# Loading the decays later and splitting one weight copy in a decayed cumulative sum over a matmul

## The chip, the cores and the metric

The kernel runs on one core of one Trainium2 chip. The metric is the device time of one execution in microseconds, the median of several runs. Matrix products run on TensorE (PE, with its weight loads shown as PEld), the rest on VectorE (DVE), ScalarE (ACT) and GpSimd (POOL). Transfers between the chip's memory and the core's on-chip memory are issued by SP, ACT or POOL, each through a queue of its own, and carried out by 16 DMA engines.

## The reference

```python
B, S, D = (16, 2048, 1024)
xw = x @ w
out[:, 0, :] = xw[:, 0, :]
for t in range(1, S):
    out[:, t, :] = decay[None, :] * out[:, t - 1, :] + xw[:, t, :]
```

A matrix product of 32,768 rows with a 1024 x 1024 matrix, then along the time of each of the 16 sequences a running sum that is multiplied in each step by a factor of its column, the decay. All arrays are float32 in the chip's memory.

## The kernel before

Time is cut into chunks of 512 steps (`TL`), 64 in all, taken two at a time. The 1024 output columns are cut into 8 tiles of 128 (`n` = 0 to 7). A step of the outer loop computes one tile for one pair of chunks: 8 products (`k` = 0 to 7) over the 1024 input columns for each chunk, in bf16, into a tile `ps` in PSUM. Then the running sum is done by DVE, either directly from PSUM ("unpaired" tiles) or, for "paired" tiles, on every other time step with the square of the decay, where ACT and POOL prepare and finish the rest. DVE turns the result back to rows in `ot`, and SP issues the stores.

x comes in by POOL's queue, cast to bf16 (`load`, tile `xb`); DVE turns it in blocks of 32 x 32 (`turn`, tile `xw`), and ACT or DVE sorts it into `xt` (`part`). The weights lie in `wsb`, indexed by `k`, by tile `n` and by 128 columns. They come in four quarters, named by half `h` (tiles 0 to 3, or 4 to 7) and by `e` (even or odd `k`). A quarter is loaded into a staging area (`load_w`), then copied in four pieces, one for each `m` with `k = 2m + e` (`settle`); a piece covers the four tiles of its half, called slots below.

Almost every instruction is held in the order in which the program writes it (`pin`). The order is written out by hand in `agenda`: a string for each step, in which a letter with a number names a deed. The entry -99 runs before the first step. Its deeds are:

- `M0` to `M3`: load half chunks of x (POOL). `U0` to `U2`: load the second to fourth quarter of w (POOL). The first quarter is loaded at the very start by SP and ACT.
- `W` and `w`: copy one piece of w on DVE or ACT. 0 to 3 are the first quarter, 4 to 7 the second (half 0, odd `k`), 8 to 11 the third, 12 to 15 the fourth.
- `K0` to `K3`: matmuls that keep PE at work and wait for x's first parts.
- `E0` to `E15`: turn a part of a half chunk (DVE), four to a half chunk; so `E8` to `E11` are the third half chunk's turn, `E12` to `E15` the fourth's. `F` and `G`: sort one part into `xt` on DVE or ACT.
- `D` (`decays`): turn the decays from `rows` into columns, copy them to `dec`, and square them into `squares`, all on DVE. `rows` is filled by a memset (L329) and four small transfers on SP (L343 to L346), near the start of the program.
- `L`: the next load of x.

The deeds around the first steps that matter here: `p0` copies tile 0 out of PSUM on ACT, `g0` multiplies every other step of tile 0 by `dec` on ACT and is the first reader of `dec`; `p2` and `g2` do the same for tile 2; `W8` to `W11` follow on DVE in step 0's entry, `w12` to `w15` on ACT behind `g2`; `S1` and `S3` are the first scans on DVE.

In step 0 the loop writes the products of the first four tiles together: first the even `k` of chunk 0 in two halves, then the odd `k` in the order `k` = 1, 3, 5, 7 and for each of them the four tiles, each product a matmul of 512 columns at L131; then chunk 1. So the first matmul that reads w's second quarter is `k` = 1 of tile 0, and the next three are tiles 1 to 3 of the same `k`, which is the piece that `W4` copies.

Of the kernel before, what the change touches and what calls it, by code (L numbers as in the profile page):

```python
# [14 lines left out]
def _ap(ap_obj: bass.AP, new_ap, extra_offset=0):  # L15
    return dataclasses.replace(
        ap_obj,
        ap=[list(p) for p in new_ap],
        offset=ap_obj.offset + extra_offset,
    )  # L20
# [5 lines left out]
def kernel(  # L26
# [26 lines left out]
    nc = tc.nc  # L53
    pin = tc.keep_in_program_order
    B, S, D = x.shape
    assert w.shape == (D, D)

    NQ = 4
    P = 32
# [6 lines left out]
    R = K // 2  # L66
    CH = D // 2
    CR = CH // NQ
# [23 lines left out]
    wcols = wsb.rearrange("p k (h r) q i -> p k h q r i", h=2)  # L92
# [48 lines left out]
    class Tile:  # L141
# [39 lines left out]
        def copy(self):  # L181
            self.xs = sb.tile([128, 2 * TL], FP32, name=f"xs{self.lot % 3}")[:, 0:self.T]
            parts = self.ps if isinstance(self.ps, tuple) else (self.ps,)
            size = self.T // len(parts)
            for i, ps in enumerate(parts):
                pin(nc.scalar.copy(out=self.xs[:, i * size:(i + 1) * size], in_=ps))  # L186
# [93 lines left out]
    class Outlet:  # L280
# [8 lines left out]
        def store(self, b, t0):  # L289
# [4 lines left out]
            for j in range(0, self.nj, nj):  # L294
# [11 lines left out]
    stage = {(0, 0): room[0][:, 0:size],  # L306
             (0, 1): room[0][:, size:size * 3 // 2].bitcast(BF16),
             (1, 0): room[1][:, 0:size // 2].bitcast(BF16),
             (1, 1): room[1][:, size // 2:size].bitcast(BF16)}
# [8 lines left out]
    def settle(h, e, m, copy):  # L318
        src = stage[h, e][:, m * CH:(m + 1) * CH]
        pin(copy(out=wcols[:, 2 * m + e, h],  # L320
                 in_=src.rearrange("p (q r i) -> p q r i", q=NQ, r=R)))
# [3 lines left out]
    rows = const.tile([128, 2, P], FP32, name="rows")  # L325
    touch = const.tile([128, 1], BF16, name="touch")
    load_w((nc.sync, nc.scalar), 0, 0)
    pin(nc.vector.memset(idle, 0.0))  # L328
    pin(nc.vector.memset(rows, 0.0))  # L329
    pin(nc.scalar.copy(out=touch, in_=idle[:, 0:1]))  # L330

    gates = [const.tile([128, 128], BF16, name=f"gate{q}") for q in range(NQ)]
# [7 lines left out]
    spin(22, idle[:, 0:128])  # L340
    H = NJ // 2
    halves = ((0, H), (H, NJ))
    for q in range(NQ):  # L343
        pin(nc.sync.dma_start(
            out=rows[q * P:q * P + R],
            in_=_ap(decay, [[P, R], [CH, 2], [1, P]], q * CR)))  # L346
    cols = const.tile([128, 2, P], FP32, name="cols")

    def load_half(i):
# [10 lines left out]
    def part_one(i, copy):  # L360
        part(i // 8, copy, i % 4, i % 4 + 1, *halves[i // 4 % 2])

    def settle_one(i, copy):
        settle(i // 8, i // 4 % 2, i % 4, copy)

    def decays(i):
        pin(nc.vector.transpose(out=cols, in_=rows))
        pin(nc.vector.tensor_copy(
            out=dec.rearrange("p (h r) -> p h r", h=2), in_=cols[:, :, 0:R]))
        square(0)  # L370
# [64 lines left out]
    def turn_and_load(c):  # L435
# [13 lines left out]
        "x": lambda c: part(c, nc.vector.tensor_copy, 0, 2),  # L449
        "y": lambda c: part(c, nc.vector.tensor_copy, 2, M),  # L450
        "W": lambda i: settle_one(i, nc.vector.tensor_copy),
        "w": lambda i: settle_one(i, nc.scalar.copy),
        "M": load_half,
        "U": load_part,
        "E": lambda i: turn(i // 8, *halves[i // 4 % 2], i % 4, i % 4 + 1),
        "F": lambda i: part_one(i, nc.vector.tensor_copy),
        "G": lambda i: part_one(i, nc.scalar.copy),
        "K": spin_on,
        "D": decays,
        "d": square_again,  # L460
        "I": identity,
# [13 lines left out]
        "L": lambda i: load(*loads.pop(0)) if loads else None,  # L475
    }
    agenda = {
        -99: "M0 M1 U0 M2 M3 U1 U2 w0 W1 w2 W3 K0 K1 K2 K3 E0 E1 G0 E2 G1 E3 F2 G3 E4 E5 G4 E6 G5 E7 F6 G7 W4 w5 W6 W7 D E8 E9 G8 E10 G9 E11 F10 G11 E12 L E13 G12 L E14 G13 E15 L F14 G15",
        0: "p0 z0 W8 W9 W10 W11",
        1: "g0",  # L480
        2: "L S1 L",
# [194 lines left out]
```

## Time and profile before

The median of three runs is 904.1 us (904.0 to 904.33). The profiled execution has a span of 902.5 us from its first to its last instruction.

| | busy us | share of the span | instructions |
|---|---|---|---|
| PE (matmuls) | 896.7 | 99% | 4201 |
| PEld (weight loads) | 411.4 | 46% | 4201 |
| DVE | 824.2 | 91% | 632 |
| ACT | 686.9 | 76% | 958 |
| POOL | 656.6 | 73% | 755 |

Busy shares are means over the whole span. In this kernel the first 30 us differ from the rest: until about 15 us the engines wait for the first transfers. The granted clock of PE is full throughout (1.00 in every stretch but the last, 0.99). Lines of the timeline give the start in microseconds from the span's start, the length, the engine, the line of the program, the operation with what it writes and reads, how many instructions are merged in the line, and in brackets the idle time before it with what ended it. SPq, POOLq and PEq are the engines' issuing parts. The stretches of the trace around the change:

| stretch, us | PE busy | DVE busy | ACT busy | POOL busy |
|---|---|---|---|---|
| 5 to 10 | 5.00 | 1.04 | 1.80 | 2.73 |
| 10 to 15 | 4.82 | 3.25 | 3.41 | 4.48 |
| 15 to 20 | 4.72 | 2.85 | 2.18 | 4.10 |
| 20 to 25 | 5.00 | 2.64 | 3.25 | 3.68 |
| 25 to 30 | 5.00 | 4.89 | 3.91 | 4.89 |

### The profile page before, as it was taken

The page shows a single profiled execution, that of the slowest core. Times are in us where ns is not written, and L with a number is a line of the kernel's source. Part 1 is how long each engine was busy: PE and PEld are TensorE (multiplying, and loading weights), DVE is VectorE, ACT ScalarE, POOL GpSimd, SP SyncE. Part 2 cuts the span into 40 slices and gives each one's busy share as a digit, 9 for nine tenths or more (in the row PEclk, how much of TensorE's full clock was granted, in tenths as well). Part 3 has the DMA queues.
Part 4 walks back from the last instruction along what each step waited for, and adds up shares of the span by engine and source line. Part 5 has one row for each costly group of instructions (what it writes and reads, how often), then busy time and mean ns, then how long its engine had stood idle before and what let it go on. Part 6 is the DMA issues. An engine that isn't in the chain of part 4 may idle for free.

```text
span 902.5 us, 12285 instructions
## 1 busy us (share of the span) xinstructions
PE 896.7 (99%) x4201; PEld 411.4 (46%) x4201; DVE 824.2 (91%) x632; ACT 686.9 (76%) x958; POOL 656.6 (73%) x755
## 2 busy tenths in 40 slices
PE   9999999999999999999999999999999999999998
PEld 5544444444444444444444444444444444444444
DVE  4999998998999999999998999999999999999998
ACT  4889867777877877878778778777787787787743
POOL 7888678777767768777677687777777776876632
PEclk9999999999999999999999999999999999999999
DMA  9999999999999999999999999999999999999858
GB/s 193 194 215 220 231 231 206 215 231 243 251 249 248 242 251 246 244 250 253 227 236 228 221 228 230 232 227 227 232 230 228 227 234 223 228 226 218 183 142 236
DMA packets 403182, 204.77 MB, mean 227 GB/s; under 512 B 9392, under 2 KB 402096, under 8 KB 403120
## 3 DMA queue, kind: packets, MB, share of 16 engines
q1 hardware_dynamic: 265808, 134.77, 60.8%
q0 software_dynamic: 137024, 68.70, 56.8%
q8 instruction: 33, 0.54, 0.2%
q10 hardware_dynamic: 288, 0.52, 0.2%
q14 instruction: 29, 0.24, 0.1%
HBM read 138.42 MB, written 134.22 MB: 302 GB/s over the span
## 4 chain that ended last, share of the span: by engine, by line
PE 98%; DMA 1%; POOL 0%; issue 0%; DVE 0%; DVEq 0%; POOLq 0%
PE ps L131 96%; PE spare L131 1%; DMA xb<-in_x_dram 1%; DMA ot<-in_w_dram 1%; POOL ot L313 0%; PE spare L398 0%; PE ps L398 0%; DVE h L416 0%; DVE wsb L320 0%; DVEq L320 0%; POOLq L660 0%
## 5 line engine op out<-in xcount | busy, mean ns | idle before, releaser
L131 PE MATMUL ps<-xt,wsb 128*128 128x512 bf16 x4016 | 866.1, 378 | 0.5 <-DVE wsb L320 0.5
L131 PEld LDWEIGHTS <-wsb 128*128 128x128 bf16 x4152 | 405.9, 98 | 479.7 <-ACT wsb L320 0.8
L208 POOL TENSOR_TENSOR xs<-h,xs 128x512 f32<-128x512 f32 (+1 forms) x190 | 242.5, 1276 | 187.1 <-ACT h L169 85.5
L186 ACT COPY xs<-ps 128x1024 f32<-128x1024 f32 (+1 forms) x190 | 188.9, 994 | 152.8 <-PE ps L131 147.7
L272 DVE STREAM_TRANSPOSE ot<-so 128x1024 f32<-128x1024 f32 (+2 forms) x264 | 300.1, 1175 | 4.5 <-DMA out_dram<-ot 2.3
L260 POOL TENSOR_TENSOR so<-h,xs 128x512 f32<-128x512 f32 (+1 forms) x190 | 241.1, 1271 | 45.2 <-ACT h L169 28.0
L123 ACT COPY xt<-xw 128x2048 bf16<-128x2048 bf16 (+1 forms) x136 | 242.2, 1789 | 7.8 <-DVE xw L115 7.8
L105 POOL DMA_DIRECT2D xb<-in_x_dram x264 | 174.0, 660 | 3.5 <-DMA ot<-in_w_dram 1.1
L169 ACT ACTIVATE h<-so,dec 128x512 f32<-128x512 f32 (+1 forms) x190 | 145.4, 766 | 29.8 <-DVE so L213 26.7
L115 DVE STREAM_TRANSPOSE xw<-xb 128x2048 f32<-128x2048 f32 (+1 forms) x78 | 147.3, 1900 | 7.0 <-DMA xb<-in_x_dram 7.0
L213 DVE TENSOR_TENSOR_SCAN so<-spare,keep,xs 128x512 f32<-128x512 f32 (+1 forms) x97 | 119.8, 1237 | 25.7 <-POOL xs L208 25.4
L213 DVE TENSOR_TENSOR_SCAN so<-spare,xs 128x512 f32<-128x512 f32 x93 | 113.1, 1218 | 26.5 <-POOL xs L208 23.6
L169 ACT ACTIVATE h<-ps,dec 128x512 f32<-128x512 f32 (+1 forms) x189 | 129.4, 685 | 0.0
L233 DVE TENSOR_TENSOR_SCAN so<-dec,ps 128x1024 f32<-128x1024 f32 x34 | 76.7, 2259 | 1.0 <-ACT h L169 1.0
L233 DVE TENSOR_TENSOR_SCAN so<-dec,keep,ps 128x1024 f32<-128x1024 f32 (+2 forms) x35 | 75.4, 2153 | 0.0
L264 ACT COPY keep<-so 128x1 f32<-128x1 f32 x136 | 25.2, 188 | 9.4 <-DVE so L233 9.0
L204 ACT COPY so<-keep 128x1 f32<-128x1 f32 x97 | 18.5, 192 | 2.7 <-DVE ot L272 2.5
L131 PE MATMUL spare<-xt,wsb 128*128 128x512 bf16 (+1 forms) x56 | 11.9, 341 | 0.0
L131 PE MATMUL ps<-xw,wsb 128*128 128x256 bf16 (+1 forms) x68 | 11.2, 301 | 0.0
L202 POOL MEMSET so<- 128x1 f32 x93 | 10.6, 116 | 0.6 <-DVE ot L272 0.6
L313 POOL DMA_DIRECT2D ot<-in_w_dram x12 | 6.5, 544 | 3.2 <-DMA xb<-in_x_dram 2.1
L338 PE MATMUL spare<-idle 128*128 128x512 bf16 x22 | 7.5, 519 | 1.2 <-DVE idle L328 1.2
(39 smaller groups left out, 39.3 us busy)
## 6 DMA issues: line engine op xcount, KB each, us to landing
out_dram<-ot SPq DMA_DIRECT2D x236, 512.0 KB, 10.9
xb<-in_x_dram POOLq DMA_DIRECT2D x248, 256.0 KB, 7.9
out_dram<-ot SPq DMA_DIRECT2D x56, 128.0 KB, 2.6
xb<-in_x_dram POOLq DMA_DIRECT2D x16, 128.0 KB, 5.8
out_dram<-ot SPq DMA_DIRECT2D x8, 256.0 KB, 4.2
ot<-in_w_dram POOLq DMA_DIRECT2D x12, 128.0 KB, 5.1
out_dram<-xb SPq DMA_DIRECT2D x3, 256.0 KB
ot<-in_w_dram ACTq DMA_DIRECT2D x2, 256.0 KB, 5.1
```

Of the source, the lines that this page charges most:

```text
L105: pin(nc.gpsimd.dma_start(out=xb_of[c][quad(q), j0:j1], in_=_ap(x, [[D, P], [P * D, j1 - j0], [1, CQ]], (b * S + t0 + j0 * P) * D + q * CQ)))
L115: pin(nc.vector.transpose(out=dst.rearrange("p (m j i) -> p j m i", m=M, i=P)[:, j0:j1, m0:m1], in_=src.rearrange("p (j m c) -> p j m c", ...
L123: pin(copy(out=xt_of[c][:, m0:m1, :, j0 * P:j1 * P], in_=src))
L131: pin(nc.tensor.matmul(out=ps[:, t0:t1] if ps.shape[1] >= t1 else ps, lhsT=lhs, rhs=rhs, start=(k == 0 and t0 == start), stop=(k == K - 1),))
L169: pin(nc.scalar.activation(out=h, in_=src, func=mybir.ActivationFunctionType.Copy, scale=dec[:, self.n:self.n + 1]))
L186: pin(nc.scalar.copy(out=self.xs[:, i * size:(i + 1) * size], in_=ps))
L208: pin(nc.gpsimd.tensor_tensor(out=odds, in0=self.g, in1=odds, op=ALU.add))
L213: pin(nc.vector.tensor_tensor_scan(out=so[:, 3:T + 2:2], data0=squares[-1][:, n:n + 1].to_broadcast([128, T // 2]), data1=self.xs[:, 1:T:2 ...
L233: pin(nc.vector.tensor_tensor_scan(out=so[:, t + 2:t + 2 + size], data0=dec[:, n:n + 1].to_broadcast([128, size]), data1=ps, initial=befor ...
L260: pin(nc.gpsimd.tensor_tensor(out=self.so[:, 2:T + 2:2], in0=self.h, in1=self.xs[:, 0:T:2], op=ALU.add))
L264: pin(nc.scalar.copy(out=self.keep, in_=self.so[:, self.T + 1:self.T + 2]))
L272: pin(nc.vector.transpose(out=outlet.ot[:, :, c0:c0 + P], in_=self.so[:, 2 + t0:2 + t0 + nj * P].rearrange("p (i t) -> p i t", t=P)))
```

## The change

Two things are changed. First, the memset of `rows` and the four transfers of the decays become a deed `N`, which stands behind `F10`, that is behind the third half chunk's turn and its part on DVE; and `D`, which works the decays out, moves from behind `W7` to behind `F14`, the fourth half chunk's part on DVE. Second, the first piece of w's second quarter, `W4`, is copied on DVE in two instructions: `q4` copies slot 0 (128 of 512 elements a partition), `Q4`, behind it on DVE, slots 1 to 3. Between them in the string stands `w5`, which is on ACT.

```diff
-    pin(nc.vector.memset(rows, 0.0))
...
-    for q in range(NQ):
-        pin(nc.sync.dma_start(
-            out=rows[q * P:q * P + R],
-            in_=_ap(decay, [[P, R], [CH, 2], [1, P]], q * CR)))
+
+    def load_decay(i):
+        pin(nc.vector.memset(rows, 0.0))
+        for q in range(NQ):
+            pin(nc.sync.dma_start(
+                out=rows[q * P:q * P + R],
+                in_=_ap(decay, [[P, R], [CH, 2], [1, P]], q * CR)))
+
...
+    def settle_slots(i, r0, r1):
+        h, e, m = i // 8, i // 4 % 2, i % 4
+        src = stage[h, e][:, m * CH:(m + 1) * CH]
+        pin(nc.vector.tensor_copy(
+            out=wcols[:, 2 * m + e, h, :, r0:r1],
+            in_=src.rearrange("p (q r i) -> p q r i", q=NQ, r=R)[:, :, r0:r1]))
...
+        "N": load_decay,
+        "q": lambda i: settle_slots(i, 0, 1),
+        "Q": lambda i: settle_slots(i, 1, R),
...
-        -99: "M0 M1 U0 M2 M3 U1 U2 w0 W1 w2 W3 K0 K1 K2 K3 E0 E1 G0 E2 G1 E3 F2 G3 E4 E5 G4 E6 G5 E7 F6 G7 W4 w5 W6 W7 D E8 E9 G8 E10 G9 E11 F10 G11 E12 L E13 G12 L E14 G13 E15 L F14 G15",
+        -99: "M0 M1 U0 M2 M3 U1 U2 w0 W1 w2 W3 K0 K1 K2 K3 E0 E1 G0 E2 G1 E3 F2 G3 E4 E5 G4 E6 G5 E7 F6 G7 q4 w5 Q4 W6 W7 E8 E9 G8 E10 G9 E11 F10 N G11 E12 L E13 G12 L E14 G13 E15 L F14 D G15",
```

The order of the instructions on PE, ACT and POOL is the same as before. On ACT, `g0` now waits for DVE itself; before, an earlier wait of ACT on DVE covered the decays.

## The prediction

> **What bounds the kernel now.** I read the chain of waits first, in order of time, because the page gives PE 99% of it and only its start and its end can hold anything else.
>
> ```profile
> 1.31 6.52 DMA xb<-in_x_dram
> ...
> 8.12 0.55 POOL ot L313
> ...
> 9.91 4.90 DMA ot<-in_w_dram
> ...
> 14.93 0.30 DVE wsb L320
> 15.23 0.05 issue
> 15.28 0.82 PE ps L131 x3
> ...
> 43.33 830.69 PE ps L131 x3848
> ```
>
> Columns are start, length, what. From 15.28 us on the chain is PE alone until the tail at 898 us: what reaches PE before 15.28 us, or stalls it later, moves the end one for one, and nothing else does. The last thing before 15.28 is one copy of w's second quarter on DVE (14.93, 0.30), which waits for the transfer that lands at 14.81; that was issued when the first x transfer had landed, at 7.84 (1.31 + 6.52).
>
> The timeline of the first 45 us comes next (start, length, engine, line, what, idle before).
>
> ```profile
> 1.66 1.35 SPq L344 DMA_DIRECT2D rows<-in_decay_dram  x4
> ...
> 14.93 0.69 DVE L320 COPY wsb<-ot 128x512 bf16<-128x512 bf16 x3 [0.85 <-DMA ot<-in_w_dram]
> ...
> 15.28 0.82 PE L131 MATMUL ps<-xt,wsb 128*128 128x512 bf16 x3 [0.46 <-DVE wsb L320]
> 15.54 0.23 DVE L367 STREAM_TRANSPOSE cols<-rows 128x64 f32<-128x64 f32 x1
> ...
> 15.81 0.17 DVE L368 COPY dec<-cols 128x8 f32<-128x8 f32 x1
> ...
> 18.99 0.39 DVE L123 COPY xt<-xw 128x512 bf16<-128x512 bf16 x1
> ...
> 20.35 1.42 DVE L115 STREAM_TRANSPOSE xw<-xb 128x256 f32<-128x256 f32 x4 [0.97 <-DMA xb<-in_x_dram]
> ...
> 24.09 1.04 DVE L320 COPY wsb<-ot 128x512 bf16<-128x512 bf16 x4 [2.01 <-DMA ot<-in_w_dram]
> ...
> 24.32 0.69 ACT L169 ACTIVATE h<-ps,dec 128x512 f32<-128x512 f32 x1
> ...
> 25.19 1.01 ACT L186 COPY xs<-ps 128x1024 f32<-128x1024 f32 x1 [0.18 <-PE ps L131]
> ...
> 28.90 1.19 PEld L131 LDWEIGHTS <-wsb 128*128 128x128 bf16 x7 [0.35 <-ACT wsb L320]
> ```
>
> To be seen: PE stands 0.46 us (14.82 to 15.28) for that copy, its only stall on real work. DVE has two holes, 0.97 us before 20.35 and 2.01 us before 24.09. The first reader of the decays, `g0` on ACT, starts at 24.32. ACT then works in a row to the four weight copies for which PE's weight loads wait until 28.90; the matmuls from 25.86 on stay 0.216 us apart (72 in 15.73), so these copies are just in time and ACT has no slack there beyond the 0.18 us of idle before 25.19.
>
> **The change, part by part.** The profiled execution has a span of 902.5 us; the runs' median of 904.1 us lies 1.6 us above it, and I take those 1.6 as unchanged.
>
> *The split copy.* `W4` (512 elements a partition) becomes `q4` (128) and `Q4` (384). Seven such bf16 copies on DVE took 283 to 428 ns, median 286; the shortest copy on DVE, 8 elements (L368), took 171. The line through these two is 0.228 ns an element, so `q4` is 0.20 us and `Q4` 0.26. PE's first matmul waits for slot 0 alone and starts 0.09 us sooner, at 15.19. The second needs `Q4`. The three copies in 0.69 us start 0.20 apart ((0.69 - 0.28) / 2); with `q4` 0.09 shorter, `Q4` starts 0.11 after it and ends at 14.93 + 0.11 + 0.26 = 15.30; with the 0.05 of issue it is ready at 15.35, and the second matmul is due at 15.19 + 0.216 = 15.41. So all 0.09 counts, with 0.06 to spare. Bounds: a `q4` as short as the memset of 64 elements (0.112) would let PE start 0.17 sooner, but `Q4` at 15.35 - 0.09 = 15.26 is then close behind, so 0.17 is the most; a `Q4` as long as the slowest copy (428 ns) is ready at 15.52, against 15.50 for the second matmul before, a loss of 0.02. I take the line, 0.09, since its ends are of this very kind of copy. `W6` and `W7` slip by 0.11 us; their matmuls come 1.7 and 2.6 us after the first, so this is covered. `w5` on ACT doesn't move.
>
> That 428 ns copy ran while POOL issued x transfers at 24.26. [...]
>
> *The decays leave the front.* Four transfers of 1 KB leave SP's queue at 1.66. In the trace's packet records they are 32 packets of 128 B, median 26 ns, at 5.21 to 6.98 us, among the first x packets, which begin at 5.28. That is 32 x 26 = 0.83 us of engine time: 0.05 us if spread over 16 engines, 0.21 if on 4. x's first landing, the transfers behind it and 14.93 come sooner by this; between 0 (a packet in a gap costs nobody) and 0.21 I take 0.05, the even spread. The memset of `rows` (0.11 us) leaves DVE at 1.10; the gates behind it are first needed at 8.31, so nothing.
>
> *`D` leaves DVE at 15.54* (transpose 0.23, copy 0.17, square 0.17, ending at 16.19). The next DVE work waits for x until 17.65: nothing.
>
> *`N`, the load.* The memset (0.11) goes into the hole from 19.38 to 20.35, covered. It releases SP at some 19.6, whose queue holds nothing until the stores at 38.79. Four issues take 1.35 us as before, the last starting near 20.6.
>
> *When they land* the trace doesn't show for this place. From below: w's first packet left SP's empty queue 1.02 us after its issue (0.75 to 1.77), so 20.6 + 1.0 + 0.1 = 21.7. Under load: the first store's first packet came at 42.59, 3.80 after its issue began, 2.14 of it the issue itself (6.42 / 3), so 1.7 after the issue's end; that puts the first decay packet at 19.6 + 0.35 + 1.7 = 21.65, and if the four then spread as before (5.21 to 7.03, 1.82 us) the last is in at 23.5. From above: the last decay transfer before took 4.3 us from issue to its end (2.7 to 7.03), giving 24.9, though w's 512 KB stood ahead in its queue; an x transfer of 128 KB takes 5.8, giving 26.4. The new place has a loaded machine but an empty SP queue, nearest to the store: I take 22.9, between the first two.
>
> [...]
>
> *`D` behind `F14`.* It can start when `F14` ends, 22.08, or when the decays land. It fills 0.65 us of the hole before 24.09. Behind it on DVE stand `W8` to `W11`, then the scans. `W8` can slip: PE needs it at 25.86 and it ends at 24.4.
>
> *The deadline.* `g0` gets a wait of its own on DVE. From landing to `dec` is 0.44 us (15.54 to 15.98) plus about 0.08 on either side, 0.60 in all. `g0` may start at 24.32 + 0.18 of ACT's idle time - 0.14 by which PE now runs sooner = 24.36. So decays that land by 23.75 cost nothing; each later microsecond is one that `g0`, the next two copies out of PSUM, `w12` to `w15` and PE lose in turn. At 22.9 there is 0.85 us of cover.
>
> Sum: -0.09 - 0.05 = -0.14 us, which gives 902.4 for the span and **903.95 us** for the time.
>
> **The rivals.**
>
> *The gain is swallowed, 904.1 us.* `Q4` comes late (the 428 ns case) or the x transfers land as before. For it: the spread of the copy's times. Against it: the median of the seven is 0.286. Its price is between -0.05 and +0.02. [...]
>
> *The decays are late, slower.* The mechanism is SP's small packets among POOL's big ones at 20 to 24 us; the place is ACT at 24.36; it decides from a landing at 23.75 on, and undoes the gain from 23.9. At 24.9 it costs 1.15 - 0.14: 905.1 us. At 26.4 it is 2.65 - 0.14: 906.6. Above 0.2% (905.9) it needs a landing at 25.7, over 5 us after the last issue. For it: the 4.3 us of the same transfer at the start. Against: that queue was full, and 1 KB is 8 packets of 26 ns.
>
> *The whole gap closes, 903.65 us.* Transfers that land sooner by the 0.21 bound and more, plus the short copy, let PE go on at 14.82. No more is there: this stall has 0.46 us, so faster by over 0.2% (below 902.3) has no mechanism in the profile.
>
> **How the numbers follow.** The forecast gets 0.58, the swallowed gain 0.15, late decays 0.19 (0.06 of it beyond 905.9), the closed gap 0.05, what I don't see 0.03. The range takes the forecast with its bounds and late decays up to the 4.3 us row: 903.6 to 905.1. A measurement of this kernel tells about 0.2% (1.8 us) from no change, so all but the far end of late decays is "the same": faster 0.02, same 0.91, slower 0.07.
>
> **What would show it.** The split: PE's stall at 15.28 shrinks from 0.46 to about 0.37, and PE's second matmul follows 0.22 after the first; a gap there is `Q4` late. The front: x's first wait ends some 0.05 sooner. The decays: the transpose of `rows` starts near 23.0 and `dec`'s copy ends before 24.3, with no idle time before `g0` put down to DVE. I am wrong if DVE waits for `rows` beyond 23.9, or if PE idles between 25.8 and 30 us.

## The result, and the profile after

The changed kernel takes 906.45 us (median of 11 runs, 905.0 to 907.81), the kernel before 904.1 us in the same comparison (903.81 to 904.48): a ratio of 1.0026, 95% interval 1.0018 to 1.0034. It is slower by 2.35 us, and its runs lie 2.8 us apart where those before lay within 0.7. The profiled execution has a span of 904.7 us, 2.2 above the 902.5 before.

The timeline of the changed kernel, with the columns as before:

```profile
14.77 0.36 DVE L372 COPY wsb<-ot 128x128 bf16<-128x128 bf16 x2 [0.84 <-DMA ot<-in_w_dram]
...
15.03 0.82 PE L131 MATMUL ps<-xt,wsb 128*128 128x512 bf16 x2 [0.35 <-DVE wsb L372]
...
19.33 1.28 SPq L346 DMA_DIRECT2D rows<-in_decay_dram  x4
...
24.56 0.24 DVE L377 STREAM_TRANSPOSE cols<-rows 128x64 f32<-128x64 f32 x1 [2.61 <-DMA rows<-in_decay_dram]
...
25.25 0.69 ACT L169 ACTIVATE h<-ps,dec 128x512 f32<-128x512 f32 x1 [1.09 <-DVE dec L378]
...
25.43 2.13 DVE L320 COPY wsb<-ot 128x512 bf16<-128x512 bf16 x4
...
25.99 1.46 PE L131 MATMUL ps<-xt,wsb 128*128 128x512 bf16 x5 [0.22 <-ACT h L169]
26.07 1.34 POOL L208 TENSOR_TENSOR xs<-h,xs 128x512 f32<-128x512 f32 x1
...
27.62 4.70 PE L131 MATMUL ps<-xt,wsb 128*128 128x512 bf16 x20 [0.17 <-DVE wsb L320]
...
29.55 2.49 PEld L131 LDWEIGHTS <-wsb 128*128 128x128 bf16 x13 [0.41 <-ACT wsb L320]
```

The same timeline some 10 us later:

```profile
36.67 2.27 DVE L115 STREAM_TRANSPOSE xw<-xb 128x2048 f32<-128x2048 f32 x1
...
40.92 1.02 PE L131 MATMUL ps<-xt,wsb 128*128 128x512 bf16 x4 [0.41 <-ACT xt L123]
...
42.73 1.02 PE L131 MATMUL ps<-xt,wsb 128*128 128x512 bf16 x4 [0.78 <-ACT xt L123]
```

In the kernel before, the lines that belong to the two readings below, POOL's first addition and chunk 2's turn, were:

```profile
26.45 1.30 POOL L208 TENSOR_TENSOR xs<-h,xs 128x512 f32<-128x512 f32 x1
...
34.24 2.27 DVE L115 STREAM_TRANSPOSE xw<-xb 128x2048 f32<-128x2048 f32 x1
```

PE's stall for the second quarter is shorter, 0.35 us, and ends at 15.03, 0.25 sooner than before. From there on it goes wrong. The decays are issued at 19.33, and DVE waits 2.61 us for them, until 24.56. ACT's `g0` starts at 25.25 where it started at 24.32. Behind the decays on DVE stand the four copies of w's third quarter; they start at 25.43 instead of 24.09, and take 2.13 us where they took 1.04, while POOL does an addition. That addition begins at 26.07, 0.38 us sooner than before, since POOL's loads ran sooner too (the one ahead of it ended at 25.98 for 26.34). And chunk 2's turn on DVE, which began at 34.24, begins at 36.67, so that PE waits for ACT's `xt` at 40.92 and 42.73, long after the decays are in.

The chain of waits of the changed kernel, in order of time (start, length, what), runs through the same places:

```profile
20.32 4.12 DMA rows<-in_decay_dram
...
24.56 0.26 DVE cols L377
...
25.43 2.13 DVE wsb L320 x4
27.56 3.32 DVE so L233 x2
...
36.75 2.20 DVE xw L115
...
40.78 1.90 ACT xt L123
...
50.23 9.88 PE ps L131 x45
```

Before, the chain was PE alone from 15.28 us; now it is the decays' transfer, then DVE until 39 us, then ACT's `xt` until 42.7, and only then PE.

How the loss divides is read from PE's weight loads, which are the same 4201 in the same order in both traces. The 131st starts 0.25 us sooner than before (23.87 against 24.12), the 161st 0.64 later (29.56 against 28.92), the 225th 2.15 later (44.88 against 42.73), the 4001st still 2.15. So 0.25 was gained by 15 us, 0.89 lost between 24 and 30 us, and 1.51 between 40 and 43: -0.25 + 0.89 + 1.51 = 2.15.

### The profile page after: what moved, and what is told of

It is laid out like the page before. It is cut to its first block, busy times and chain, and to the rows that moved or that the text cites. A ratio compares the mean times of both kernels' runs of the same rounds, so it can differ in the third digit from the quotient of the medians.

```text
span 904.7 us, 12204 instructions
## 1 busy us (share of the span) xinstructions
PE 892.3 (99%) x4119; PEld 410.8 (45%) x4201; DVE 826.1 (91%) x633; ACT 686.4 (76%) x958; POOL 656.5 (73%) x755
## 4 chain that ended last, share of the span: by engine, by line
PE 94%; DMA 2%; DVE 2%; issue 1%; POOL 0%; ACT 0%; SPq 0%; DVEq 0%; POOLq 0%
PE ps L131 93%; DMA xb<-in_x_dram 1%; PE spare L131 1%; DVE so L233 1%; DMA rows<-in_decay_dram 0%; DVE xw L115 0%; POOL ot L313 0%; DVE wsb L320 0%; ACT xt L123 0%; POOL xb L105 0%; DVE ot L272 0%; DVE so L213 0%; PE spare L408 0%; PE ps L408 0%; SPq L346 0%
```

## The experiments

Each was compared with the kernel before on its own chip, whose medians there were 904.32 (first four), 904.37 (next four) and 904.47 us (last three). "Moved" and "split" below are the two halves of the change.

**The split alone.** The agenda of before, with `q4 w5 Q4` for `W4 w5`:

```diff
-... G7 W4 w5 W6 W7 D E8 ...
+... G7 q4 w5 Q4 W6 W7 D E8 ...
```

> Only the split copy; the decays are loaded and worked out where they were before. Theory (the loss is all in the late decays; the split alone gives PE its 0.09 us): 904.0 us, 0.1 below before, PE's stall for the first piece of the second quarter some 0.09 us shorter. Rival (the split harms the copies behind it): above before.

904.22 us against 904.32, ratio 0.9998 (0.9989 to 1.0007). The split does no harm, and a gain of 0.1 us can't be told from none by the time. The traces can tell it a little better: from the start of the first copy to the first matmul behind it, it took 0.35 us before, 0.25 in the changed kernel and 0.31 here.

**The move alone.** The changed kernel with `W4` whole:

```diff
-... G7 q4 w5 Q4 W6 W7 E8 ...
+... G7 W4 w5 W6 W7 E8 ...
```

> Only the decays are moved, the copy is whole. Theory (late decays): the whole loss is here, 906.0 to 907.0 us, with DVE's transpose of the decays waiting for their transfers until about 24.5 us and runs that scatter over 1 us and more. Rival (loss from the split): 904.0.

907.83 us (906.5 to 908.21), ratio 1.0035 (1.0022 to 1.0047): the whole loss is here, and more than expected. Its timeline shows where the rest comes from:

```profile
25.14 3.73 DVE L320 COPY wsb<-ot 128x512 bf16<-128x512 bf16 x4
...
26.21 1.30 POOL L208 TENSOR_TENSOR xs<-h,xs 128x512 f32<-128x512 f32 x1
...
27.45 1.30 POOL L105 DMA_DIRECT2D xb<-in_x_dram  x2
28.76 1.30 POOL L208 TENSOR_TENSOR xs<-h,xs 128x512 f32<-128x512 f32 x1
...
28.93 12.71 PE L131 MATMUL ps<-xt,wsb 128*128 128x512 bf16 x58 [1.77 <-DVE wsb L320]
```

The four copies of the third quarter take 3.73 us; they end 0.12 us after POOL has done an addition and two issues of x loads in a row. The same copies as one group of the tile `wsb` (minimum, median and maximum in ns, then first and last start), in the kernel before, the changed one, and here:

```profile
L320 DVE COPY wsb<-ot x4: 286/290/428, 24.1 to 24.7; 128x512 bf16<-128x512 bf16 x4
```

```profile
L320 DVE COPY wsb<-ot x4: 275/359/1376, 25.4 to 26.2; 128x512 bf16<-128x512 bf16 x4
```

```profile
L320 DVE COPY wsb<-ot x4: 274/300/3091, 25.1 to 25.8; 128x512 bf16<-128x512 bf16 x4
```

One copy of the four, the last, is stretched from 0.29 us to 1.38 or 3.09. Before, the copies ran while POOL only issued loads, and ended at 25.13, well before POOL's addition at 26.45. In the changed kernel the meeting is close: the addition begins at 26.07, the last copy at 26.2, and without the hold the copies would have ended near 26.47 (an estimate, 25.43 + 1.04).

**The load in front, the work late.** The decays are loaded as before, `D` stands behind `F14`, the copy is whole:

```diff
-... W6 W7 D E8 ...  ... L F14 G15
+... W6 W7 E8 ...  ... L F14 D G15
```

> The decays are loaded at the front as before, but worked out behind the fourth half chunk's turn; the copy is whole. Theory (what costs is the landing, not the place of the three instructions on DVE): 904.1 us, no change, runs within 0.7 us. Rival (0.65 us of work in that hole of DVE's delays the third quarter's copies): 904.5 and more.

904.18 us, ratio 0.9999 (0.9990 to 1.0008), runs 903.98 to 905.29. The place of the three instructions costs nothing that the time shows; what costs is the landing.

**The load earlier.** The changed kernel with `N` behind `W7`:

```diff
-... Q4 W6 W7 E8 E9 G8 E10 G9 E11 F10 N G11 ...
+... Q4 W6 W7 N E8 E9 G8 E10 G9 E11 F10 G11 ...
```

> The whole change, but the load stands right behind the second quarter's copies, some 3.6 us earlier on DVE. Theory (late landing): the transfers land near 20 us, before the transpose can start at 22, so nothing waits, and what is left is the split and the empty front: 903.85 us, 0.25 below before. Rival (small transfers among the big ones take longer the earlier they are issued, since more is queued, and land at the same time as in the changed kernel): 906 us.

904.16 us against 904.32 (runs 903.78 to 904.5), ratio 0.9996 (0.9987 to 1.0005). The loss is gone, and of the gain that is left 0.16 us is seen, which can't be told from none. From its timeline:

```profile
15.76 1.29 SPq L346 DMA_DIRECT2D rows<-in_decay_dram  x4
...
21.90 0.23 DVE L377 STREAM_TRANSPOSE cols<-rows 128x64 f32<-128x64 f32 x1
...
24.09 0.69 ACT L169 ACTIVATE h<-ps,dec 128x512 f32<-128x512 f32 x1
```

The transpose has no idle time before it. The packet records put the decays' packets at 19.15 to 20.71 us, 3.4 to 4.95 after the first issue; in the changed kernel it was 22.48 to 23.94, 3.15 to 4.6 after it. The delay goes with the issue, and is no property of one place.

**The decays behind the weight copies.** The changed kernel with `D` taken from behind `F14` and set behind `W11`; the load stays late:

```diff
-0: "p0 z0 W8 W9 W10 W11",
+0: "p0 z0 W8 W9 W10 W11 D",
```

> The whole change, but the decays are worked out on DVE behind W8 to W11 instead of ahead of them; the load stays late. Theory (the decays' lateness costs PE 0.9 us by way of ACT, and all beyond that comes from what stands behind the wait on DVE): W8 to W11 run near 24 us in about 1 us as before, g0 starts no sooner than 25.2, and the time is 904.6 to 905.2 us. Rival (the wait of ACT alone makes the loss, whatever DVE does): 906.0 and more.

905.21 us (904.82 to 905.99), ratio 1.0009 (1.0000 to 1.0018): 0.84 us above before, at the upper end of what was expected.

```profile
24.68 1.04 DVE L320 COPY wsb<-ot 128x512 bf16<-128x512 bf16 x4 [2.27 <-DMA ot<-in_w_dram]
...
25.64 0.23 DVE L377 STREAM_TRANSPOSE cols<-rows 128x64 f32<-128x64 f32 x1
...
26.30 0.69 ACT L169 ACTIVATE h<-ps,dec 128x512 f32<-128x512 f32 x1 [1.58 <-DVE dec L378]
...
27.03 16.25 PE L131 MATMUL ps<-xt,wsb 128*128 128x512 bf16 x70 [0.71 <-ACT h L169]
```

The copies take 1.04 us again, although `g0` starts a whole microsecond later than in the changed kernel (PE itself was some 0.5 us later here by its 131st weight load). PE never waits for `xt`. The trace is of the slowest of the 11 runs, 905.99: in it PE loses 1.39 us between its 131st and 161st weight loads and nothing behind them. By the medians, then, the wait on ACT makes 0.84 of the 2.35 us at most, less than half, and the rest comes from what stands behind the wait on DVE.

**The load later still.** `N` behind `E13`:

```diff
-... F10 N G11 E12 L E13 G12 ...
+... F10 G11 E12 L E13 N G12 ...
```

> The whole change, with the load two pieces of the fourth half chunk's turn later on DVE, some 1.7 us. Theory (PE loses what the landing is late, one for one): the transpose of the decays starts near 26.2 us and the time is 907.5 to 909 us. Rival (the landing is set by POOL's big transfers and not by the issue): 906.5, the same as the changed kernel.

908.05 us (five runs, 906.61 to 908.22), ratio 1.0036 (1.0024 to 1.0049). The transpose starts at 26.91, 2.35 later than in the changed kernel for an issue 1.71 later (21.04 against 19.33). The number came out as expected, yet not by that theory alone: the copies here escape POOL's addition (the longest takes 0.29 us), although the last of them began at 28.19, beside an addition that began at 28.17; there it is the addition that took longer, 1.45 us for 1.30. And something new appears. PE stands idle for 2.42 us until 28.14. The stretches after it follow; a line gives the stretch, its length, the busy time and number of instructions of PE, PEld, DVE, ACT and POOL, and then PE's granted clock (0.57 in the first line):

```profile
28.00:29.00 1.00, 0.64 (x2) 0.33 (x4) 1.00 (x4) 1.00 (x3) 0.83 (x1) 0.57 1.44 194
29.00:30.00 1.00, 1.00 (x3) 0.40 (x3) 1.00 (x1) 1.00 (x3) 1.00 (x2) 0.50 1.46 198
30.00:31.00 1.00, 1.00 (x4) 0.30 (x2) 1.00 (x2) 1.00 (x3) 0.99 (x3) 0.50 1.45 197
31.00:32.00 1.00, 1.00 (x5) 0.41 (x4) 0.89 (x2) 0.73 (x3) 1.00 (x1) 0.72 1.44 195
32.00:33.00 1.00, 1.00 (x6) 0.46 (x5) 1.00 (x1) 0.00 (x0) 1.00 (x3) 1.00 1.44 194
```

PE ran at half its clock until 31.5 us. So this run is no clean measure of the slope from landing to time.

**POOL's addition out of the way.** The changed kernel with `j0`, the first addition, behind POOL's next two loads of x. Nothing else moves in the program:

```diff
-3: "p2 z2 L g2 j0 S3 w12 w13 L w14 L w15 k1",
+3: "p2 z2 L g2 S3 w12 w13 L w14 L w15 j0 k1",
```

> The whole change, with POOL's first addition (j0) moved behind POOL's next two loads of x. Theory (the last of the third quarter's copies on DVE is held up by POOL's addition, since the late decays push the copy into it): no copy there takes over 0.6 us, DVE's first scan starts near 26.5 instead of 27.5, runs scatter less, and the time is 905.0 to 905.8 us. Rival (DVE is late by the wait alone, the long copy only shows it): 906.5 and the same long copy.

905.32 us (905.05 to 905.76), ratio 1.0011 (1.0002 to 1.0020). Against the kernel before it loses 0.95 us where the changed kernel lost 2.35, and its runs are 0.7 us apart instead of 2.8. The same group of copies:

```profile
L320 DVE COPY wsb<-ot x4: 275/341/422, 25.7 to 26.5; 128x512 bf16<-128x512 bf16 x4
```

No copy is held, DVE's first scan starts at 26.81 instead of 27.48, and yet the decays land no sooner (the transpose starts at 25.08). In this trace, of the slowest of the 11 runs, PE still waits 0.4 us for `xt`. The kernel before with `j0` later was not run, so what that move is worth without late decays is not known.

**One transfer of four.** The changed kernel with `for q in range(1)` in `load_decay`: three quarters of the decays stay zero.

> The whole change, but only the first of the four transfers of the decays is made: three quarters of the decays are left at zero. Theory (the wait under load before the first packet and the spread of the four add up to the late landing): the one transfer is in near 22.9 us, the transpose starts by 23.4, and the time is 903.7 to 904.3 us. Rival (the whole delay is before the first packet): the transpose starts at 24.2 or later and the time is 905.5 and more.

904.26 us against 904.37, ratio 0.9999 (0.9991 to 1.0008). From its timeline:

```profile
19.71 0.30 SPq L346 DMA_DIRECT2D rows<-in_decay_dram  x1
...
23.80 0.25 DVE L377 STREAM_TRANSPOSE cols<-rows 128x64 f32<-128x64 f32 x1 [1.55 <-DMA rows<-in_decay_dram]
...
24.40 0.69 ACT L169 ACTIVATE h<-ps,dec 128x512 f32<-128x512 f32 x1
24.46 0.90 DVE L320 COPY wsb<-ot 128x512 bf16<-128x512 bf16 x4
```

The transpose came later than expected (23.80, not 23.4), 4.1 us after the issue, and still all is well: `g0` is on time, and the copies end at 25.36, before POOL's addition. A landing 0.76 us sooner than in the changed kernel (23.80 against 24.56) is worth 2.5 us of time (2.35 lost there, 0.11 gained here, each against the kernel before on its chip). So the loss is not one for one; around here it is much steeper.

**Three on one chip.** The changed kernel and the move alone once more, and the move alone with `j0` later:

> The changed kernel once more, on one chip with the next two. Theory (the loss above 1 us hangs on how long POOL shuts out the last of the third quarter's copies, which differs from run to run): 905.5 to 907.5 us with runs 2 us apart, and in the profile the last copy's length again far from 0.29 us. Rival (scatter of the landing alone): runs within 1 us.

> The decays moved, the copy whole, once more. Theory (the split matters by its 0.1 us only, and the larger loss of the first such run came from the chip and the collision): within 0.7 us of the changed kernel's median on this chip. Rival (the split takes a microsecond off the loss): 1 us or more above it.

> The decays moved, the copy whole, and POOL's first addition (j0) behind its next two loads of x. Theory (POOL's addition and not the split decides): 905.2 to 905.9 us, runs within 1 us, no copy of the third quarter over 0.6 us. Rival: as the kernel with the decays moved alone.

The changed kernel again: 906.78 us (905.01 to 908.03), ratio 1.0026 (1.0017 to 1.0036); its last copy took 1.38 us. The move alone: 906.51 us (905.13 to 907.73), ratio 1.0024 (1.0013 to 1.0035), last copy 1.52 us. So the split makes no difference that the time shows, and the 1.2 us by which the move alone seemed worse at first do not come from it; whether the chip or scatter made them is not shown. With `j0` later: 905.38 us, ratio 1.0016 (1.0007 to 1.0025), but one run of 906.51 and one of 908.86 beside nine from 904.99 to 905.81. The profiled execution is the one of 908.86, with a span of 907.1 us:

```profile
25.29 1.91 POOL L105 DMA_DIRECT2D xb<-in_x_dram  x3
...
25.58 4.39 DVE L320 COPY wsb<-ot 128x512 bf16<-128x512 bf16 x4
...
27.29 2.53 POOL L208 TENSOR_TENSOR xs<-h,xs 128x512 f32<-128x512 f32 x2
...
30.03 12.71 PE L131 MATMUL ps<-xt,wsb 128*128 128x512 bf16 x58 [2.43 <-DVE wsb L320]
```

Here the last copy began 0.68 us before POOL's first addition (26.61 against 27.29), during the last issue of x, and was held for 3.37 us until both additions were done. So the copy need not begin inside an addition to be held. Over all traces, each copy of this group that was held for more than a microsecond ended behind at least one addition, and those beside load issues alone took at most 0.52 us. Expected was that no copy would be held; that failed. The long copy beside POOL's work is seen again, and nine runs of eleven below 905.9 suggest that the remedy made the meeting rarer, without showing it.

## Why the prediction was wrong

- *The range and the sign.* 906.45 lies above the range (903.6 to 905.1), and the likeliest case was not what happened. The rival of late decays, which had 0.19, happened, with its mechanism and its place on ACT, but cost more than it was priced. Two steps failed: the landing, which turned the forecast into its rival, and the work behind the wait on DVE, which took the time out of the range. By this trace the landing alone would have cost some 0.89 - 0.25 = 0.64 us, an estimate, and 904.7 lies within the range.
- *"When they land": mis-sized by 1.5 us.* I took 22.9; the chain has the transfer ending at 24.44 and DVE going on at 24.56. The bounds of that step (21.7 to 24.9) held. The value was chosen by the wrong part of the row: the first store's wait was split into its own long issue and 1.7 us after it, and the 1.7 taken over. The first decay packet came 3.15 us after the first issue (22.48 - 19.33), close to the store's whole 3.80, and DVE went on 0.6 us after the last packet, for which I had put some 0.1. The spread of the four was nearly right: 1.46 us against 1.82.
- *The deadline and ACT's price: right in mechanism, and close in size partly by luck.* By that step a landing at 24.44 costs 24.44 - 23.75 = 0.69 over the forecast's deadline; with the 0.11 us that PE was ahead beyond the forecast's 0.14 it is 0.80. Measured between 24 and 30 us: 0.89. From landing to `g0` it took 0.81 us (24.44 to 25.25), not 0.60, chiefly since `dec`'s copy took 0.38 us for 0.17; counted from `g0` the same step would have given 1.00.
- *"`W8` can slip: PE needs it at 25.86": this is the step that took the time out of the range.* It priced what is queued behind the wait on DVE by PE's need of `W8` alone, and gave it no term in the rival: it was put at nothing. Two things were left out. The slip of 1.34 us (25.43 against 24.09) moved the four copies into POOL's addition, beside which they took 2.13 us for 1.04 in this trace. (The copy that came late was `W11`, not `W8`: PE stood 0.17 us for it at 27.62, and 1.77 and 2.43 us in the two traces with the longest holds.) And DVE has nothing to catch up with: before, from 30 to 40 us it was busy for 10.00 of 10.00 us. The two together, 1.34 + 1.09 = 2.43 us, are just what chunk 2's turn slipped (36.67 against 34.24), and 1.51 us of them reached PE at 41 to 43 us, at its two waits for `xt`. The runs bear it out: with the copies ahead of the wait 0.84 us is lost, with the addition moved 0.95, with neither 2.35. The two remedies were not run together.
- *A slow copy beside POOL's work: weighed in the wrong place.* The prediction had the 428 ns copy beside POOL's issues, and used it as a bound for the split at 15 us alone, where nothing of the kind happened in the changed kernel's trace: `Q4` took 0.25 us. It bears on the copies behind `D`, where it was not weighed: there the last one took 1.38 us against 0.29 and ended 0.15 us after POOL's addition. The copy of 3.09 us lasted through three of POOL's instructions; why it did not end between them is open.
- *The split: right in size, where the copy ran undisturbed.* `q4` took 0.20 us and `Q4` 0.25, as the line gave; PE went on 0.25 us behind the copy's start for 0.35 before, 0.10 sooner for 0.09 predicted. In four of the eight traces with the split it was so; in the other four `q4` took 0.26 to 0.31 us, and PE went on after 0.31 to 0.37. (The whole copy had such a case too: 0.43 us, PE after 0.49, in the run with the load in front and the work late.) PE's second matmul came 0.23 us after the first (by its weight load, 15.26 against 15.03), so `Q4` was not late.
- *The empty front: not settled.* The first matmul of the second quarter starts at 15.28, 15.52 and 15.10 us in three traces with the decays in front, and at 15.03, 15.02 and 15.05 in the first three without, but at up to 15.57 in later ones. A gain of 0.05 is below this scatter.
- *"No mechanism for faster": right.* The best version, with the load earlier, is 0.16 us below before, within its interval.

## What to carry to other kernels

A wait that is put on an engine must be priced by all that the program holds behind it there (here the four copies, 1.34 us late), and followed until that engine has idle time again; on DVE, busy without a gap for the next 15 us, 2.4 us of delay came out at PE some 16 us later as 1.5 us of loss. Ask too what the delayed instructions will now run beside: here a copy that had ended just before another engine's work was pushed into it and grew from 0.3 to 1.4 us and more, so that 0.8 us of landing decided about 2.5 us of time. A small load on a loaded machine took 4.1 us (one of 1 KB) or 5.0 to 5.9 us (four of 1 KB) from issue to use here, where the engine waited for it; issued 3.6 us sooner it cost nothing.

## What the runs showed of the hardware

- A transfer of 1 KB from an empty queue, with POOL's transfers under way, took 2.6 to 3.4 us to its first packet in the ten traces in which the load stood behind the start (22.48 - 19.33 in the changed kernel, 22.46 - 19.88 and 19.15 - 15.76 at the ends), where w's first packet on the idle machine took 1.02.
- A bf16 copy of 512 elements on DVE, 0.29 us alone, took 1.38, 1.52, 3.09 and 3.37 us beside POOL's additions and load issues. It ended each time 0.12 to 0.16 us after one of POOL's instructions did. Whether the copy is held, and for how long, may be why the runs scatter: with the addition out of the way, 11 runs lay within 0.7 us, but in the second such kernel two of 11 stood out, and the one of these that was profiled had the longest hold. That every longer run had such a copy is not shown, since only one execution of each kernel was profiled.
- PE idle for 2.42 us came back at half its clock (0.50) for some 3.4 us (28.14 to 31.5) when the load was latest; after 2.43 us of idle in the last experiment it came back at full clock (1.00 from 30 to 34 us). What decides between them is open.
